# A depthwise convolution shared between the matrix engine and the vector engine

## The chip, the cores and the metric

The kernel runs on one core of a Trainium2 chip. A core has five engines with a queue of instructions each: TensorE (PE in the profile, its weight loads PEld), VectorE (DVE), ScalarE (ACT), GpSimd (POOL) and SyncE (SP), which here issues nearly all DMAs. Each queue runs in order, and engines wait for one another through semaphores. [...] The metric is the device time of one execution in microseconds; lower is better.

## The reference

A two-layer decoder trunk with width 2048, 256 positions, batch 1, all in float32:

```
layer 0: x <- LN(a*x + (1+gt)*S5(x*(1+sc)+sh));    x <- LN(a*x + (1+gt)*FFN(...))
layer 1: x <- LN(a*x + (1+gt)*Conv(x*(1+sc)+sh));  x <- LN(a*x + (1+gt)*FFN(...))

Conv(u):  ab = u @ w_pw1                      # 2048 -> 4096
          v  = ab[:, :D] * sigmoid(ab[:, D:])
          v[t, d] = sum_{k<31} v[t-30+k, d] * w_dw[k, d] + b_dw[d]   # causal, each channel alone
          v  = LayerNorm(v) ; return silu(v) @ w_pw2
FFN(u):   (silu(u @ w_g) * (u @ w_u)) @ w_down                      # 2048 -> 5632 -> 2048
```

The vectors sh, sc and gt, six per layer, come from a conditioning vector: `silu(c) @ ada_w[i] + ada_b[i]`, a matrix of 2048 x 12288 per layer. The change touches the 31-tap convolution in `Conv`, the LayerNorm behind it, and the time at which the products with `ada_w` are made.

## The kernel before

Activations lie with channels on the 128 partitions, in 16 chunks of 128 channels by 256 positions. A matmul in float32 precision is made of three faster ones: weights and activations are each split into a rounded part and the rest (`whi`, `wlo`; `hh`, `hl`), and hi x hi, hi x lo and lo x hi are summed. Weights arrive in units of four 128-row blocks by 512 columns (class `Unit`): SyncE loads `raw` (four buffers in all), ScalarE casts it to `whi` (L830), VectorE subtracts to make `wlo` (L831), PE multiplies (L886 with 512 output columns, L890 with 256). `gemm` runs one such unit after another; each is 24 or 48 matmuls.

**Modulation.** Most of `ada_w` goes through VectorE, not PE. A queue (`AdaQueue`) has one step per block: SyncE loads 1 MB into one of the same four buffers (`rawa`, L684), and VectorE adds it, times a column of `silu(c)`, to a running sum (`adaacc`, L699). Each unit of a gemm adds `ada.rate` to a credit; a whole credit starts a step, unless `ada.hold` is set. The credit starts at -3 behind a stage's first panel and never passes 1.5. `ada.finish` makes all steps that a vector still lacks. What remains of the last vector is made on PE (`ada_block`, L628).

**Convolution stage.** Eight gated gemms (i = 0 to 7) each yield two chunks, 2i and 2i+1. Gemms 0 to 6 come out with positions on partitions and are turned by PE (L902); the last one comes out with channels on partitions. `conv_in` copies both chunks with 30 zero columns ahead of them into `pad`, one of two tiles for pairs. PE has no operation per channel, so the convolution is put as matmuls over four shifted copies: SyncE writes `pad` to DRAM (`scr`, L1576) and reads it back four times (`conv_copies`, L1591) into `vs`, in which 32 channels stand four times, shifted by 0 to 3 positions. For the last gemm PE and two copying engines make `vs` without DRAM (`conv_spread`, L1598 to L1602). GpSimd makes the matching weights `lw` (L1581), 32 x 32 diagonals. `conv_out` then issues, for each chunk, 8 groups of 4 taps x 4 quarters of 32 channels (L1608: 32 matmuls in the program, 64 in the profile), and VectorE moves the result out of PSUM into `V`, with the bias added and the shift of the LayerNorm subtracted (L1617).

`Stats` collects the sums of `V` and of its squares: ScalarE squares (L764), VectorE adds both to running sums pair by pair (L773, L775); `finish` sums over partitions on PE (L790, L794), makes the inverse deviation on VectorE and spreads it on PE (L809). A stage opened with `apart` leaves the last pair out of the running sums and keeps it as `tail`.

**Swish.** `Feed` then drives the first gemm of `w_pw2`: for each pair, VectorE normalises (L818, L819), ScalarE makes the sigmoid (L1645) and the affine form (L947), GpSimd multiplies them (L1647), VectorE rounds the product to `hh` (L910, in `split3`), GpSimd makes the rest `hl` (L911). For the first pair VectorE does all but the rest (L1634 to L1638).

**Order of the work.** `later.put(n, f)` calls f when n further units have begun, so the program's text order interleaves convolution work with weight units. That order is not yet the queues' order: a planner with a cost model fills each engine's queue, taking what is ready in its model and, among that, what was written first. So work written later can be moved ahead. Only some PE stretches are set by hand, and `queue_behind` ties instructions behind a given one. `later.flush` behind gemm 7 calls all that is still due.

Of the kernel before, what the change touches and what calls it, by code (L numbers as in the profile page):

```python
# [11 lines left out]
F32 = mybir.dt.float32  # L12
# [14 lines left out]
CONV_G = 8  # L27
WIDTH = 31
# [477 lines left out]
def kernel(  # L506
# [231 lines left out]
    class Stats:  # L738
# [22 lines left out]
        def add(self, i, z):  # L761

            sq = self.sp.tile([P, 2, SEQ], F32, tag="lnsq", name="lnsq", bufs=2)
            act = nc.scalar.activation(out=sq, in_=z, func=AF.Square)  # L764
# [7 lines left out]
            a, b = self.first if i == 1 else (s[:, 0], s[:, 1])  # L772
            dve = nc.vector.tensor_tensor(out=s[:, 0], in0=a, in1=z, op=ADD)  # L773
            if i < 7:
                nc.vector.tensor_tensor(out=s[:, 1], in0=b, in1=sq, op=ADD)  # L775
            else:
                self.tail = sq
                self.marks = [dve, act]

        def finish(self, fill=None):  # L780
# [4 lines left out]
            sp, s, sq = self.sp, self.s, self.tail  # L785
# [5 lines left out]
            for k in range(2):  # L791
                for q in range(4):
                    t = slice(64 * q, 64 * q + 64)
                    mm = nc.tensor.matmul(b[32 * q:32 * q + 32, 64:P], ones[:, 0:32], sq[:, k, t], start=False, stop=k == 1)  # L794
# [113 lines left out]

    def split3(src, hi, lo):
        a = nc.vector.tensor_copy(out=hi, in_=src)  # L910
        nc.gpsimd.tensor_tensor(out=lo, in0=src, in1=hi.bitcast(F32), op=SUB)  # L911
        return [a]
# [596 lines left out]
    with mctx:  # L1509
# [39 lines left out]
        ada.rate, ada.behind = 0.71, True  # L1549
# [11 lines left out]
        for p in pad:  # L1561
            nc.vector.memset(p[:, :, :WIDTH - 1], 0.0)
            nc.vector.memset(p[:, :, LP - 1:], 0.0)
        dramp = cvctx.enter_context(tc.tile_pool(name="dram", bufs=1, space=bass.MemoryType.DRAM))
        scr = [dramp.tile([P, 2, LP], F32, name=f"scr{i}") for i in range(7)]
        cstats = Stats("cln", sp)
        ada.rate = 0.6

        def conv_in(i, t):
            p = pad[i % 2]  # L1570
            for k in range(2):
                nc.scalar.copy(out=p[:, k, WIDTH - 1:LP - 1].rearrange("p (c t) -> p t c", t=2), in_=t[:, k].rearrange("p (t c) -> p t c", t=2))
            vs = cp.tile([P, 2, 4, LS], F32, tag="vs", name="vs", bufs=2)
            wait = {0: 5, 7: 2}.get(i, 6)
            if i < 7:
                later.put(wait - 3, lambda: nc.sync.dma_start(scr[i], p))  # L1576
                later.put(wait - 2, lambda: conv_copies(scr[i], vs))
            for k in range(2):
                ch = 2 * i + k
# [3 lines left out]
                    in1=bc(wtap[:, :, 4 * ch:4 * ch + 4].rearrange("p g q -> p q g"), 3, 32), op=MUL)  # L1583
                if i == 7:
                    later.put(1 + k, lambda k=k: conv_spread(p[:, k], vs[:, k]))
                later.put(wait + k, lambda ch=ch, k=k, lw=lw: conv_out(ch, vs[:, k], lw))
# [125 lines left out]
```

## Time and profile before

| | us |
|---|---|
| median of three runs | 2320.72 |
| lowest and highest | 2317.39, 2323.02 |
| the profiled execution, its own time | 2323.75 |
| its span, first to last instruction | 2322.0 |

The stages that matter in its trace: feed-forward of layer 0 until about 1140 us from the start of the span, convolution from 1178 to 1438, its LayerNorm and swish until 1484, the rest of `w_pw2` until 1560, feed-forward of layer 1 behind that.

A row of groups reads: line, engine, operation, output <- inputs, shapes, count | busy us, mean ns of one | idle us just ahead of them, and what ended it. A row of the timeline reads: start us, duration us, engine, line, operation, count, and in brackets the idle time ahead and its releaser.

### The profile page before, as it was taken

The numbers are of one execution on the slowest core, as the hardware profiler recorded it, in microseconds if no ns is written. First come the engines' busy times: TensorE is split into PE (matmuls) and PEld (weight loads), VectorE is DVE, ScalarE is ACT, GpSimd is POOL, SyncE is SP. The second block draws the span as 40 slices with busy tenths as digits, with TensorE's granted clock in tenths as the row PEclk, the third lists the DMA queues.
The fourth block names the chain that finished last, engine by engine and source line by source line (L and its number), as shares of the span: only waits on it lengthen the run. The fifth ranks groups of instructions, "written<-read, shape, count | busy, mean of one in ns | idle before, by whom it ended". The sixth has DMA issues, their size and how long they took to land.

```text
span 2322.0 us, 33968 instructions
## 1 busy us (share of the span) xinstructions
PE 2249.4 (97%) x13905; PEld 1811.9 (78%) x13905; DVE 1633.0 (70%) x1778; ACT 1011.1 (44%) x1242; POOL 186.6 (8%) x283
## 2 busy tenths in 40 slices
PE   6888999999999999999999998999999999999998
PEld 4545778988888888888897676798888888888888
DVE  8899878887777777777885565788754544555564
ACT  4666335554333334344453322556434333334343
POOL 5662000000000000000011111400000000000000
PEclk9999999999999999999999999999999999999999
DMA  9889799589888898988757886766865556555542
GB/s 334 289 301 302 268 320 337 168 304 323 294 321 294 314 318 294 324 293 318 274 164 222 265 241 193 276 223 206 275 218 187 193 182 197 184 182 189 191 164 91
DMA packets 382307, 582.35 MB, mean 251 GB/s; under 512 B 13604, under 2 KB 279124, under 8 KB 367684
## 3 DMA queue, kind: packets, MB, share of 16 engines
q1 hardware_dynamic: 381718, 579.73, 73.8%
q8 instruction: 109, 1.79, 0.3%
q0 software_dynamic: 192, 0.37, 0.1%
q14 instruction: 48, 0.39, 0.0%
q10 hardware_dynamic: 240, 0.08, 0.0%
HBM read 575.97 MB, written 4.15 MB: 250 GB/s over the span
## 4 chain that ended last, share of the span: by engine, by line
PE 82%; DVE 8%; DMA 4%; ACT 3%; issue 1%; POOL 1%; SPq 0%; DVEq 0%; ACTq 0%; POOLq 0%
PE acc L886 67%; PE acc L890 5%; PE conv L1608 2%; DVE wlo L831 2%; PE acc L1007 2%; PE turned L902 2%; DMA raw<-in_cv_w_pw_dram 1%; DMA raw<-in_s_w_glu_dram 1%; ACT whi L830 1%; DVE pin L462 1%; PE y L499 1%; PE ada L628 1%; DMA raw<-in_ada_w_dram 1%; DVE adaacc L699 1%; DVE x L450 0%
## 5 line engine op out<-in xcount | busy, mean ns | idle before, releaser
L831 DVE TENSOR_TENSOR wlo<-raw,whi 128x2048 fp32r<-128x2048 f32 x344 | 795.6, 2313 | 491.0 <-ACT whi L830 490.6
L830 ACT CAST whi<-raw 128x2048 fp32r<-128x2048 f32 x344 | 655.0, 1904 | 805.0 <-PE acc L886 579.1
L886 PE MATMUL acc<-whi,h 128*128 128x512 f32 x3648 | 895.0, 395 | 10.8 <-ACT whi L830 10.5
L886 PEld LDWEIGHTS acc<-whi,h 128*128 128x128 f32 x3648 | 679.4, 188 | 169.7 <-ACT whi L830 16.4
L886 PE MATMUL acc<-wlo,h 128*128 128x512 f32 x1824 | 466.1, 392 | 2.8 <-DVE wlo L831 2.8
L886 PEld LDWEIGHTS acc<-wlo,h 128*128 128x128 f32 x1824 | 341.6, 188 | 81.3 <-DVE wlo L831 6.7
L886 PE MATMUL acc<-whi,f 128*128 128x512 f32 x1248 | 300.5, 391 | 0.0
L699 DVE SCALAR_TENSOR_TENSOR adaacc<-rawa,c_act,adaacc 128x2048 f32<-128x2048 f32 (+1 forms) x135 | 284.5, 2108 | 0.4
L886 PEld LDWEIGHTS acc<-whi,f 128*128 128x128 f32 x1248 | 233.0, 188 | 48.9 <-ACT whi L830 0.8
L886 PE MATMUL acc<-wlo,f 128*128 128x512 f32 x624 | 156.4, 389 | 0.0
L886 PEld LDWEIGHTS acc<-wlo,f 128*128 128x128 f32 x624 | 117.1, 188 | 24.3
L1581 POOL TENSOR_TENSOR lw<-fold,wtap 128x1024 f32<-128x1024 f32 x16 | 33.7, 2110 | 1146.4 <-PE acc L890 926.4
L628 PE MATMUL ada<-raw,c_rep 128*32 128x512 f32 (+1 forms) x576 | 72.5, 600 | 5.7 <-DMA raw<-in_ada_w_dram 3.2
L1240 ACT ACTIVATE fsg<-acc 128x256 f32<-128x256 f32 x84 | 31.7, 380 | 100.0 <-PE acc L886 100.0
L890 PEld LDWEIGHTS acc<-h,whi 128*128 128x128 f32 x512 | 62.1, 190 | 8.1 <-DVE h L1637 2.6
L890 PE MATMUL acc<-h,whi 128*128 128x256 f32 x512 | 65.7, 283 | 2.6 <-DVE h L1637 1.7
L1184 POOL CAST lnmh<-lno 128x2 fp32r<-128x2 f32 x1 | 0.2, 183 | 829.3 <-DVE lno L66 829.3
L1608 PE MATMUL conv<-vs,lw 128*32 128x256 f32 x1024 | 59.8, 380 | 0.0
L1608 PEld LDWEIGHTS conv<-vs,lw 128*32 128x32 f32 x1024 | 36.7, 110 | 20.9 <-issue 3.0
L1241 DVE TENSOR_TENSOR fsg<-acc,fsg 128x256 f32<-128x256 f32 x84 | 35.1, 420 | 19.9 <-ACT fsg L1240 19.8
L462 DVE TENSOR_TENSOR_SCAN pin<-rho,pin 128x256 f32<-128x256 f32 x64 | 44.3, 692 | 1.5
L1617 DVE SCALAR_TENSOR_TENSOR V<-conv,vec,shift 128x256 f32<-128x256 f32 x14 | 9.7, 693 | 48.8 <-PE conv L1608 48.8
(331 smaller groups left out, 1829.8 us busy)
## 6 DMA issues: line engine op xcount, KB each, us to landing
raw<-in_ffn_w_gu_dram SPq DMA_DIRECT2D x352, 512.0 KB, 4.5
rawa<-in_ada_w_dram SPq DMA_DIRECT2D x128, 1024.0 KB, 5.9
raw<-in_ffn_w_down_dram SPq DMA_DIRECT2D x88, 1024.0 KB, 5.1
raw<-in_ada_w_dram SPq DMA_DIRECT2D x64, 1024.0 KB, 7.8
raw<-in_s_w_glu_dram SPq DMA_DIRECT2D x64, 512.0 KB, 6.0
raw<-in_cv_w_pw_dram SPq DMA_DIRECT2D x64, 512.0 KB, 6.3
raw<-in_cv_w_pw_dram SPq DMA_DIRECT2D x16, 1024.0 KB, 5.6
vs<-scr SPq DMA_DIRECT2D x28, 284.0 KB, 7.4
```

The lines of the kernel that those rows point to most:

```text
L462: v.tensor_tensor_scan(out=z, data0=rh[:, a].rearrange("p r h c -> p (r h c)"), data1=z, initial=0.0, op0=MUL, op1=ADD)
L628: nc.tensor.matmul(acc[32 * (k % 4):32 * (k % 4) + 32, :], c_rep[:, kk, :], r[:, k, :], start=kk < 4, stop=kk >= NCH - 4)
L699: nc.vector.scalar_tensor_tensor(out=acc, in0=r[:, i], scalar=c_act[:, kk:kk + 1], in1=acc, op0=MUL, op1=ADD)
L830: m1 = nc.scalar.copy(out=self.hi[:, :kn], in_=r[:, :kn])
L831: m2 = nc.vector.tensor_tensor(out=self.lo[:, :kn], in0=r[:, :kn], in1=self.hi[:, :kn].bitcast(F32), op=SUB)
L886: nc.tensor.matmul(acc[bank].rearrange("p a b -> p (a b)"), x[:, bank * HALF:(bank + 1) * HALF], wt[:, k], start=first, stop=end)
L890: nc.tensor.matmul(acc[bank][:, i], wt[:, k, m * P:(m + 1) * P], x, start=first and i == 0, stop=end and i == 1)
L902: nc.tensor.transpose(b[:, o:o + HALF], u[t][:, c0 + k * P:c0 + (k + 1) * P], ident)
L1007: nc.tensor.matmul(acc[m][:, 0:EW], wt[:, k, m * P:(m + 1) * P], xx[:, 4 * u + k], start=u == 0 and n == 0, stop=u == 3 and n == len(order ...
L1241: nc.vector.tensor_tensor(out=t[:, i], in0=gv[:, 0], in1=t[:, i], op=MUL)
L1581: nc.gpsimd.tensor_tensor(out=lw, in0=fold32.unsqueeze(1).unsqueeze(1).broadcast_to([P, 4, CONV_G, 32]), in1=bc(wtap[:, :, 4 * ch:4 * ch + ...
L1608: nc.tensor.matmul(acc[32 * q:32 * q + 32, :], lw[:, q, g, :], vs[:, q, 4 * g:4 * g + SEQ], start=g == 0, stop=g == CONV_G - 1)
```

## The change

Chunks 3, 7, 11 and 13 are no longer convolved by PE; VectorE sums their 31 taps. Of chunk 15, PE keeps the first 2 of 8 groups (taps 0 to 7) and VectorE sums taps 8 to 30.

- `conv_taps` multiplies a shifted view of the padded chunk by a column of 31 tap weights and adds it to one of two alternating sums (`vacc` and the chunk's place in `V`), joins the two and subtracts the shift. The taps are handed out with `later`: 4 per unit for i = 1 and 3, 7 for i = 5, 9 for i = 6, all 23 at once for i = 7.
- For i = 1, 3 and 5 the tap chunk has a pad tile of its own (`vpad`, two of them), because its taps run on for eight units (five for i = 5). Only the other chunk of such a pair goes through DRAM. `vs` is now one tile per chunk, three buffers, where it was one per pair, two buffers; `conv_copies` issues four reads per chunk.
- The tap columns are loaded by GpSimd's queue at the stage's start (five pieces), turned by PE after five units, and lie in the stage's own pool, which closes with the stage.
- `cstats` is opened with `apart`; `there` adds a pair to the statistics when both its chunks are done, in whatever order. `finish` takes a tail of one or two tiles.
- In `swish`, GpSimd's product and rest move to VectorE; the rounding copy moves from VectorE to ScalarE for pairs 1 to 7 (`split` in place of `split3`).
- `ada.rate` goes from 0.71 to 0.77 in feed-forward 0 and from 0.6 to 0.25 in the convolution, where the queue is also held for gemms 6 and 7.

The core of the diff:

```diff
+V_CHUNKS = (3, 7, 11, 13, 15)
+V_FROM = 8
...
-        ada.rate, ada.behind = 0.71, True
+        ada.rate, ada.behind = 0.77, True
...
-        cstats = Stats("cln", sp)
-        ada.rate = 0.6
+        cstats = Stats("cln", sp, True)
+        ada.rate = 0.25
...
+        for n, cs in enumerate((V_CHUNKS[:4], V_CHUNKS[4:])):
+            r = rows_in("taps", [cv_w_dw[0][:, P * c:P * c + P] for c in cs], nc.gpsimd)
+            later.put(5, lambda n=n, cs=cs, r=r: tap_columns(n, cs, r))
...
-            vs = cp.tile([P, 2, 4, LS], F32, tag="vs", name="vs", bufs=2)
+            ch = 2 * i
+            mine = ch + 1 in V_CHUNKS
+            vs = [cp.tile([P, 4, LS], F32, tag="vs", name="vs", bufs=3) for _ in range(1 if mine and i < 7 else 2)]
             wait = {0: 5, 7: 2}.get(i, 6)
...
+            acc = cp.tile([P, SEQ], F32, tag="vacc", name="vacc", bufs=2)
+            todo = list(range(V_FROM if i == 7 else 0, WIDTH))
+            n = {5: 7, 6: 9, 7: 23}.get(i, 4)
+            for m in range(0, len(todo), n):
+                later.put(1 + m // n, lambda js=todo[m:m + n]: conv_taps(ch + 1, acc, z[1], js, todo[0], js[-1] == WIDTH - 1))
...
+        def conv_taps(ch, acc, z, js, begin, last):
+            w, sums = taps[ch], (acc, V[:, ch])
+            for j in js:
+                a = sums[j % 2]
+                if j == begin:
+                    nc.vector.tensor_scalar(out=a, in0=z[:, j:j + SEQ], scalar1=w[:, j:j + 1], scalar2=cb_col[:, ch:ch + 1], op0=MUL, op1=ADD)
+                elif j == begin + 1:
+                    nc.vector.tensor_scalar(out=a, in0=z[:, j:j + SEQ], scalar1=w[:, j:j + 1], scalar2=None, op0=MUL)
+                else:
+                    nc.vector.scalar_tensor_tensor(out=a, in0=z[:, j:j + SEQ], scalar=w[:, j:j + 1], in1=a, op0=MUL, op1=ADD)
+            if not last:
+                return
+            nc.vector.tensor_tensor(out=acc, in0=acc, in1=V[:, ch], op=ADD)
...
+        def conv_rest(vs, lw):
+            acc = aux("conv")[:, :SEQ]
+            conv_groups(acc, vs, lw, V_FROM // 4)
+            o, a, b = V[:, 15].rearrange("p (t c) -> p c t", t=2), *(x.rearrange("p (c t) -> p c t", t=2) for x in (acc, tail[0]))
+            nc.vector.tensor_tensor(out=o, in0=a, in1=b, op=ADD)
+            there(15)
+
+        def there(ch):
+            done.add(ch)
+            if ch ^ 1 in done:
+                cstats.add(ch // 2, V[:, ch & ~1:(ch | 1) + 1])
...
             for j in range(4):
-                nc.sync.dma_start(vs[32 * j:32 * j + 32], s[:, :, j:j + LS].rearrange("(q r) k t -> r k q t", q=4))
+                for k, v in enumerate(vs):
+                    nc.sync.dma_start(v[32 * j:32 * j + 32], s[:, k, j:j + LS].rearrange("(q r) t -> r q t", q=4))
...
         for i in range(8):
+            ada.hold = i > 5
...
-            nc.gpsimd.tensor_tensor(out=h, in0=h, in1=V[:, s2], op=MUL)
-            return [m1] + split3(h, hh[:, s2], hl[:, s2])
+            nc.vector.tensor_tensor(out=h, in0=h, in1=V[:, s2], op=MUL)
+            return split(h, hh[:, s2], hl[:, s2])
```

More of the change, by code (lines that the diff above doesn't have):

```diff
@@ L907, in split @@
         return a, nc.vector.tensor_tensor(out=lo, in0=src, in1=hi.bitcast(F32), op=SUB)
[L909 to L912, printed above, removed]
     class Feed:
@@ new lines, in conv_in @@
+                if k == 1 and mine:
+                    later.put(4, lambda v=v, lw=lw: conv_rest(v, lw))
+                else:
+                    later.put(wait + k, lambda k=k, v=v, lw=lw: conv_out(ch + k, v, lw))
+            if not mine:
+                return
[4 more added lines that the diff above has]
+                later.put(1 + m // n, lambda js=todo[m:m + n]: conv_taps(ch + 1, acc, z[1], js, todo[0], js[-1] == WIDTH - 1))
@@ L1661 @@
         feed = Feed(cstats, swish, fill())
+        ada.hold = False
         ada.finish(1, 2)
```

68 lines of the change are left out of this document (42 added, 26 removed).

## The prediction

> **What bounds the kernel now.** I read the page first, then the busy time by stage, then the groups and the chain of waits of the convolution and of the LayerNorm behind it.
>
> ```profile
> span 2322.0 us, 33968 instructions
> PE 2249.4 (97%) x13905; PEld 1811.9 (78%) x13905; DVE 1633.0 (70%) x1778; ACT 1011.1 (44%) x1242; POOL 186.6 (8%) x283
> ```
>
> TensorE is busy nearly everywhere, but not evenly. The windows view gives, for each stretch, its length, the busy time of PE, PEld, DVE, ACT and POOL, the granted TensorE clock, the DMA share and GB/s.
>
> ```profile
> 420.00:1140.00 720.00, 719.62 (x3360) 592.79 (x3359) 557.74 (x429) 303.40 (x268) 0.00 (x0) 1.00 0.85 298
> 1182.00:1382.00 200.00, 192.56 (x1376) 144.72 (x1375) 128.78 (x118) 82.11 (x103) 21.29 (x10) 1.00 0.76 228
> 1382.00:1438.00 56.00, 50.68 (x648) 41.60 (x646) 26.43 (x26) 13.39 (x18) 5.93 (x3) 1.00 0.72 216
> 1416.00:1438.40 22.40, 19.54 (x320) 14.47 (x320) 7.12 (x13) 3.89 (x9) 1.97 (x1) 1.00 0.55 111
> 1437.00:1440.00 3.00, 1.56 (x39) 1.01 (x42) 1.59 (x4) 0.79 (x2) 0.00 (x0) 0.85 0.03 5
> 1440.00:1444.00 4.00, 4.00 (x32) 1.22 (x24) 2.77 (x13) 0.00 (x0) 0.00 (x0) 0.68 0.42 115
> ...
> 1437.00:1484.00 47.00, 38.53 (x307) 28.52 (x308) 32.09 (x58) 25.09 (x39) 25.43 (x16) 0.93 0.71 249
> 1484.00:1560.00 76.00, 76.00 (x463) 66.78 (x461) 65.92 (x78) 37.52 (x43) 0.00 (x0) 1.00 0.72 251
> ```
>
> The first row is the feed-forward of layer 0: PE has no gap. The convolution (1182 to 1438) and the stage that feeds its result to the next matmul (1437 to 1484) have gaps: 7.4, 5.3 and 8.5 us. VectorE has room in the convolution: 26.4 of 56 us at its end, while the last row shows PE without a gap beside a VectorE that is 87% busy. So here PE's work is the bound, then the gaps.
>
> **Taps: what leaves PE.** The groups of the convolution (1178 to 1437) and single rows of the timeline:
>
> ```profile
> L831 DVE TENSOR_TENSOR wlo<-raw,whi 128x2048 fp32r<-128x2048 f32 x32 | 80.2, 2509 | 30.5 <-ACT whi L830 30.5
> ...
> L1608 PE MATMUL conv<-vs,lw 128*32 128x256 f32 x1024 | 59.8, 380 | 0.0
> L830 ACT CAST whi<-raw 128x2048 fp32r<-128x2048 f32 x31 | 58.9, 1901 | 58.5 <-DMA raw<-in_cv_w_pw_dram 36.1 <-PE acc L886 13.4 <-PE acc L1007 5.5
> L886 PE MATMUL acc<-wlo,h 128*128 128x512 f32 x192 | 49.7, 396 | 2.6 <-DVE wlo L831 2.6
> ...
> L1046 DVE SCALAR_TENSOR_TENSOR sg<-lnrep,ecol,sg 128x256 f32<-128x256 f32 x4 | 1.7, 477 | 0.0
> ```
> ```profile
> 1215.00 0.87 DVE L1046 SCALAR_TENSOR_TENSOR sg<-lnrep,ecol,sg 128x256 f32<-128x256 f32 x2
> ...
> 1301.26 2.13 PE L886 MATMUL acc<-wlo,h 128*128 128x512 f32 x8 [0.49 <-DVE wlo L831]
> ...
> 1310.52 2.12 PE L886 MATMUL acc<-whi,h 128*128 128x512 f32 x8 [1.64 <-ACT whi L830]
> ...
> 1318.50 3.95 PE L886 MATMUL acc<-whi,h 128*128 128x512 f32 x16 [1.59 <-ACT whi L830]
> ...
> 1356.89 7.11 PE L1608 MATMUL conv<-vs,lw 128*32 128x256 f32 x128
> ```
>
> Two chunks take 128 matmuls in 7.11 us, so one costs 3.55 us of PE. Chunks 3, 7, 11 and 13 leave whole, chunk 15 keeps 2 of its 8 groups: 4.75 chunks, 16.9 us. Chunks 3 and 7 lie wholly in the stretch up to 1382, where PE sets the pace: **7.1 us off**.
>
> The price is on VectorE: 4 x 31 + 23 = 147 taps, nearly all scalar_tensor_tensor of 128x256. The L1046 row is the same form (SBUF in, scalar column, summed in place): 0.48 us each, but two in 0.87, so a new one starts each 0.40 us. 147 x 0.40 = 59 us; if each waited for the one before it, 147 x 0.48 = 71 us. The two alternating sums leave no tap waiting for its neighbour, so I take 0.40.
>
> **Room for them.** The modulation sums (adaacc) leave the stage. Their queue's credit rule, walked through the loops, gives 79 steps in feed-forward 0 and 13 in the convolution, as the trace has them:
>
> ```profile
> L684 SPq DMA_DIRECT2D rawa<-in_ada_w_dram x79: 340/341/341, 451.7 to 1120.9; - x79
> L699 DVE SCALAR_TENSOR_TENSOR adaacc<-rawa,c_act,adaacc x74: 2341/2345/2349, 481.6 to 1135.2; 128x2048 f32<-128x2048 f32 x74
> ...
> L684 SPq DMA_DIRECT2D rawa<-in_ada_w_dram x13: 340/546/2676, 1209.8 to 1381.0; - x13
> ```
>
> With the new rates the same walk gives 89 and 2; about as many as before follow later (13 against 12). The convolution loses 11 x 2.34 = 26 us of VectorE and 11 loads of 1 MB from SyncE's queue. Those loads share four buffers with the weights. Both 1.6 us gaps above are PE waiting for a cast that waited for a late weight load; with the buffers freer I take **2 us** of these 3.2. Against it, taps queue ahead of wlo: PE already waits 0.49 us for wlo at 1301, so a batch of four (1.6 us) can cost that where it meets a busy VectorE. Bounds +4 to -4 us of gain. On SyncE's queue 40 column copies of one chunk replace 28 of two, 12 issues more beside 11 loads less: nothing. GpSimd, idle for most of the stage, makes 12 of the 16 weight tiles lw and issues five small loads ahead of them, and VectorE clears two more pads: nothing that PE waits for.
>
> In feed-forward 0 the ten extra sums are 23 us in 720 on an engine 77% busy: 81%, below the 87% at which PE ran without a gap. Ten loads of 1 MB raise 298 GB/s by some 15. That cover is what hides them: **0**, and 23 us if it were gone.
>
> **The last matmul and what follows (1382 to 1438).**
>
> ```profile
> 1416.86 0.43 DVE L1093 TENSOR_TENSOR sg<-acc,sg 128x256 f32<-128x256 f32 x1 [0.76 <-ACT sg L1092]
> ...
> 1417.84 0.45 DVE L1602 COPY vs<-spread 128x284 f32<-128x284 f32 x1 [0.56 <-PE spread L1598]
> ...
> 1436.24 0.66 DVE L1617 SCALAR_TENSOR_TENSOR V<-conv,vec,shift 128x256 f32<-128x256 f32 x1 [2.76 <-PE conv L1608]
> 1436.94 0.63 ACT L764 ACTIVATE lnsq<-V 128x512 f32<-128x512 f32 x1 [6.25 <-DVE V L1617]
> ...
> 1437.60 0.69 DVE L775 TENSOR_TENSOR cln_s<-cln_s,lnsq 128x512 f32<-128x512 f32 x1
> 1438.44 0.65 PE L790 MATMUL lnsum<-cln_s,ones 128*32 128x128 f32 x16 [2.23 <-DVE cln_s L775]
> ```
>
> Today PE works through the last chunks after the gate's last product (ends 1417.3); the sums begin at 1438.4. PE loses 2.75 chunks here, 9.8 us, but VectorE becomes the limit. Behind 1417.3 it owes 23 taps (9.2), their closing sum and shift (0.34 + 0.69), the join of chunk 15 (0.69), four copies (4 x 0.45), two results (2 x 0.69) and two sums (2 x 0.69): 15.5 us, so 1432.8 instead of 1438.3, 5.5 us earlier. If the last 13 taps of chunk 13 (5.2 us) are still owed, nothing is left. I take 1.5 here, and 2.5 of chunk 11's 3.55 us, since its and chunk 13's taps fill VectorE in the last matmul: **4 us**, with PE's 9.8 as the upper bound. The lower one: 35 taps come due in the four units of the last matmul and 36 behind it, 71 x 0.40 = 28.4 us, plus 1.9 of closings; VectorE is idle 29.6 us in this stretch. Where no gap takes them, they lie on the path: see the first rival.
>
> The last pair's statistics no longer pass VectorE (0.69 x 2 give way to a square of 0.63 and eight matmuls like the 0.65 us row's), and the columns cost PE two transposes, which I put at the size of that row as well: **-0.5** together.
>
> **The swish stage (1437 to 1484).** GpSimd's product and residue go to VectorE, the rounding copy to ScalarE.
>
> ```profile
> L911 POOL TENSOR_TENSOR h<-hf,h 128x512 fp32r<-128x512 f32 x7 | 13.1, 1870 | 3.8 <-DVE h L910 3.8
> L1647 POOL TENSOR_TENSOR hf<-hf,V 128x512 f32<-128x512 f32 x7 | 11.1, 1580 | 1.2 <-ACT V L947 1.2
> ...
> L1645 ACT ACTIVATE hf<-V,vec 128x256 f32<-128x256 f32 x14 | 7.7, 594 | 7.3 <-POOL h L911 5.2 <-DVE V L819 2.1
> L947 ACT ACTIVATE V<-V,vec 128x256 f32<-128x256 f32 x14 | 7.7, 589 | 0.0
> ...
> L819 DVE TENSOR_TENSOR V<-V,lnrep 128x512 f32<-128x512 f32 x7 | 4.8, 685 | 0.1
> L818 DVE TENSOR_TENSOR V<-V,lnrep 128x512 f32<-128x512 f32 x7 | 4.8, 680 | 0.0
> L910 DVE CAST h<-hf 128x512 fp32r<-128x512 f32 x7 | 3.0, 427 | 10.5 <-POOL hf L1647 10.5
> ```
> ```profile
> 1452.19 1.27 POOL L1647 TENSOR_TENSOR hf<-hf,V 128x512 f32<-128x512 f32 x1 [1.17 <-ACT V L947]
> ...
> 1476.60 3.28 POOL L911 TENSOR_TENSOR h<-hf,h 128x512 fp32r<-128x512 f32 x1 [0.54 <-DVE h L910]
> ...
> 1478.77 1.19 PE L890 MATMUL acc<-h,wlo 128*128 128x256 f32 x8 [1.46 <-DVE wlo L831]
> ```
>
> GpSimd is the slowest link: seven pairs from 1452.2 to 1479.9, 24.2 us of it busy. Afterwards a pair costs ScalarE 0.59 x 4 + 0.63 (the square of this size) = 3.0 us by durations (2.6 with the overlap of neighbours, as in the 0.87 row) and VectorE four operations of 0.68 (2.4 to 2.7). Seven pairs and three weight casts of 1.9: 24 us from 1450, so the last residue stands at about 1475 instead of 1479.9. PE has work beside it, so I take **3 us**; bounds 6 and, as VectorE gains 7.5 us of work in front of the wlo that PE waits 1.46 us for, -2.
>
> **The sum** against the execution's own 2323.75 us: 7.1 + 2 + 4 - 0.5 + 3 = 15.6, so 2308.1. That execution lies 3.0 above the median of the runs, so against 2320.72 it is **2305 us**.
>
> **The rivals.** *The taps land on the path of the last matmul.* VectorE's queue runs in order. In gemm 7 each wlo that PE waits for stands behind up to 12 taps, and behind it chunk 15's result stands behind what is left of chunk 13's. At worst 14.0 us (35 taps) delay wlo; behind the product come 36 taps and closings (16.3) on top of today's chain, less two results and their waits (2 x 0.69 + 2 x 2.76 = 6.9): 9.4. Together 23.4, against gains of 7.1 + 3.55 + 2 + 3 = 15.6: 7.8 slower, **2328 us**. It decides from the point where more than 39 of those 71 taps stand before something that PE waits for. For it: waits on conv like the 2.76 us one already hold VectorE there. Against it: 29.6 us idle, 4.7 more without two modulation sums, and a planner that moves ready work forward.
>
> *The gaps take all of it:* PE's 16.9 us, 4 of waits, 5 in the swish stage: 26, **2295 us**. For it stands VectorE's room, against it the tail's 15.5 us.
>
> *The weights set the pace:* the cast waits 36.1 us for loads. If matmuls come to wait where PE did convolution, the 7.1 and the 4 go, swish alone remains, less its half: **2319 us**. Against it: 11 MB of loads less.
>
> *A cold array.* PE idles 1.4 us of the three in 1437 to 1440 and is then granted 0.68.
>
> ```profile
> 1439.10 5.34 PE L628 MATMUL ada<-raw,c_rep 128*32 128x512 f32 x32
> ```
>
> If VectorE's tail leaves PE idle for longer, these 32 matmuls run at half clock: 5.34 x 0.68 / 0.5 = 7.3, 2 us more, and lnrep behind them 1 more: **2308 us**. [...]
>
> **How the numbers follow.** Chances: forecast 0.55, taps on the path 0.15, gaps take all 0.11, weights 0.11, cold array 0.08. Faster by over 0.2% (4.6 us, about what a measurement of this kernel tells from no change): forecast, full gain and cold array, plus a little of the weights' case, 0.76; within, 0.10; slower, 0.14. The range reaches from the full gain, 2295, to just short of the weights' case, 2317.
>
> **What would show it.** The conv group falls from 1024 matmuls to 720 and from 59.8 us to about 43. The tap line shows 147 operations of 0.48 us or less. adaacc counts 2 in the convolution and 89 before it. PE's gaps in the stretch that was 1182 to 1382 stay at or below 7.4 us, and the stretch is some 9 us shorter. From gemm 7's first unit to lnsum it takes about 52 us; 60 or more and the first rival holds. In the swish stage POOL is idle and the last residue comes some 3 to 5 us earlier. The forecast is wrong if PE's waits for wlo in the convolution exceed the 2.6 us of today's group by more than 5, or if feed-forward 0 shows PE gaps.

## The result, and the profile after

The changed kernel takes **2300.04 us** (median of four runs, 2298.67 to 2303.70) against 2320.21 (2317.39 to 2323.02) for the kernel before: a ratio of 0.9916, with a 95% interval from 0.9898 to 0.9933. The forecast was 2305 with a range from 2295 to 2317. The total was near; the table shows that its parts were not, so that the total came so near is in part luck.

The page of the kernel after begins so:

```profile
span 2299.0 us, 33563 instructions
PE 2230.6 (97%) x13619; PEld 1798.1 (78%) x13619; DVE 1691.5 (74%) x1945; ACT 1015.0 (44%) x1249; POOL 156.6 (7%) x268
```

I cut both traces at the same landmarks: the first matmul of feed-forward 0's and of the convolution's entry panel, the first unit of gemm 7 (the first weight matmul with 256 columns), `lnsum`, and the first `shift` matmul behind the swish stage. The windows view has the columns of the prediction; first before, then after:

```profile
419.50:1171.10 751.60, 751.22 (x3619) 624.12 (x3618) 578.03 (x453) 318.35 (x283) 0.00 (x0) 1.00 0.84 295
1171.10:1382.58 211.48, 203.53 (x1486) 155.12 (x1485) 140.26 (x129) 86.64 (x109) 27.77 (x13) 1.00 0.73 218
1382.58:1438.40 55.82, 50.10 (x645) 41.14 (x643) 26.15 (x26) 13.39 (x18) 5.93 (x3) 1.00 0.70 213
```
```profile
416.10:1176.70 760.60, 756.44 (x3631) 623.13 (x3630) 597.94 (x464) 318.44 (x284) 0.00 (x0) 1.00 0.88 306
1176.70:1369.36 192.66, 191.16 (x1348) 151.03 (x1346) 157.88 (x221) 88.28 (x109) 21.52 (x10) 1.00 0.69 201
1369.36:1416.90 47.54, 41.60 (x472) 31.60 (x469) 40.78 (x80) 11.84 (x17) 5.39 (x2) 0.96 0.33 105
```

| stage, us | before | after | change | forecast |
|---|---|---|---|---|
| S5 layer and what lies ahead (code not changed) | 419.5 | 416.1 | -3.4 | 0 |
| feed-forward 0 | 751.6 | 760.6 | **+9.0** | 0 |
| convolution up to gemm 7 | 211.5 | 192.7 | **-18.8** | -9.1 |
| gemm 7 to `lnsum` | 55.8 | 47.5 | **-8.3** | -3.5 |
| LayerNorm and swish | 45.0 | 44.3 | -0.7 | -3 |
| rest of `w_pw2`, feed-forward 1 | 838.6 | 837.8 | -0.8 | 0 |

The first row moves with every execution: over the profiles of this study, whose code there is the same, it lies between 411.4 and 419.5. The changes in the table add up to -23.0 us, by the medians it is -20.2. So a stage difference of a few us in one execution says little by itself; the medians decide.

Two errors of opposite sign nearly cancel: feed-forward 0 pays 9 us that I had put at nothing, and the convolution gains 27.1 us where the forecast had 12.6. The waits of ScalarE's weight casts in feed-forward 0 (us in total, times, longest), before and after, show a change of kind:

```profile
ACT whi L830 <- DMA raw<-in_ffn_w_down_dram: 13.5, 4, 4.7
...
ACT whi L830 <- DMA raw<-in_ffn_w_gu_dram: 6.0, 2, 4.3
```
```profile
ACT whi L833 <- DMA raw<-in_ffn_w_gu_dram: 158.4, 55, 6.2
...
ACT whi L833 <- DMA raw<-in_ffn_w_down_dram: 66.0, 21, 5.9
```

Before, a cast waited for a load in 6 cases; after, it does in 76. Yet PE is marked busy for 756.4 of 760.6 us. Matmul ends are modelled in these profiles, so I take it that a slightly late start need not show as idle: of the 9.0 us only 3.8 appear as more idle time, and PE's busy time grows by 5.2. Of these, 1.6 are 12 more matmuls, which sum up the extra modulation steps (`adar` 5.3 us against 4.3, `adat` 3.0 against 2.4); the other 3.6 come with the same work. Here **the stage's length and the casts' waits** tell what the busy share hides.

The convolution's groups after the change:

```profile
L834 DVE TENSOR_TENSOR wlo<-raw,whi 128x2048 fp32r<-128x2048 f32 x32 | 74.6, 2333 | 21.4 <-ACT whi L833 21.3
...
L833 ACT CAST whi<-raw 128x2048 fp32r<-128x2048 f32 x32 | 60.9, 1904 | 63.0 <-PE acc L889 34.9 <-issue 12.1 <-PE acc L1005 5.6
L889 PE MATMUL acc<-wlo,h 128*128 128x512 f32 x192 | 48.8, 391 | 0.0
L1667 PE MATMUL conv<-vs,lw 128*32 128x256 f32 x720 | 43.4, 390 | 2.5 <-DVE V L1680 2.0 <-DVE vs L1662 0.4
...
L701 DVE SCALAR_TENSOR_TENSOR adaacc<-rawa,c_act,adaacc 128x2048 f32<-128x2048 f32 x2 | 4.7, 2346 | 0.0
```

The row of L833 shows where a part of the gain comes from: the cast, which waited 36.1 us for weight loads, now waits mainly for PE to free its buffer. PE waits nowhere for wlo in the wide gemms (0.0 in the row of L889).

### The profile page after: what moved, and what is told of

Same layout as the page of the kernel before. It is cut to its first block, busy times and chain, and to the rows that moved or that the text cites. A ratio compares the mean times of both kernels' runs of the same rounds, so it can differ in the third digit from the quotient of the medians.

```text
span 2299.0 us, 33563 instructions
## 1 busy us (share of the span) xinstructions
PE 2230.6 (97%) x13619; PEld 1798.1 (78%) x13619; DVE 1691.5 (74%) x1945; ACT 1015.0 (44%) x1249; POOL 156.6 (7%) x268
## 4 chain that ended last, share of the span: by engine, by line
PE 71%; DVE 14%; DMA 8%; ACT 5%; issue 2%; SPq 0%; DVEq 0%; ACTq 0%
PE acc L889 57%; PE acc L893 5%; DMA raw<-in_ffn_w_gu_dram 4%; DVE wlo L834 4%; ACT whi L833 3%; DMA raw<-in_ffn_w_down_dram 2%; PE acc L1005 2%; DVE adaacc L701 2%; PE conv L1667 1%; PE turned L905 1%; DVE pin L464 1%; PE y L501 1%; DMA raw<-in_s_w_glu_dram 1%; PE ada L630 0%; DVE x L452 0%
## 5 line engine op out<-in xcount | busy, mean ns | idle before, releaser
L834 DVE TENSOR_TENSOR wlo<-raw,whi 128x2048 fp32r<-128x2048 f32 x344 | 789.1, 2295 | 465.1 <-ACT whi L833 462.2
L833 ACT CAST whi<-raw 128x2048 fp32r<-128x2048 f32 x344 | 655.2, 1905 | 821.4 <-PE acc L889 447.1
L889 PE MATMUL acc<-whi,h 128*128 128x512 f32 x3648 | 895.5, 394 | 5.4 <-ACT whi L833 5.1
L889 PEld LDWEIGHTS acc<-whi,h 128*128 128x128 f32 x3648 | 677.8, 188 | 164.6 <-ACT whi L833 12.7
L889 PE MATMUL acc<-wlo,h 128*128 128x512 f32 x1824 | 465.5, 392 | 0.8 <-DVE wlo L834 0.6
L889 PEld LDWEIGHTS acc<-wlo,h 128*128 128x128 f32 x1824 | 341.9, 188 | 78.1 <-DVE wlo L834 3.4
L889 PE MATMUL acc<-whi,f 128*128 128x512 f32 x1248 | 301.1, 391 | 0.1
L889 PEld LDWEIGHTS acc<-whi,f 128*128 128x128 f32 x1248 | 232.7, 188 | 50.1 <-ACT whi L833 2.2
L889 PE MATMUL acc<-wlo,f 128*128 128x512 f32 x624 | 156.6, 389 | 0.2 <-DVE wlo L834 0.2
L889 PEld LDWEIGHTS acc<-wlo,f 128*128 128x128 f32 x624 | 117.0, 188 | 24.9 <-DVE wlo L834 0.6
L1594 POOL TENSOR_TENSOR lw<-fold,wtap 128x1024 f32<-128x1024 f32 x12 | 26.9, 2249 | 1060.5 <-PE acc L893 870.9
L1667 PE MATMUL conv<-vs,lw 128*32 128x256 f32 x720 | 43.4, 390 | 2.5 <-DVE V L1680 2.0
L464 DVE TENSOR_TENSOR_SCAN pin<-rho,pin 128x256 f32<-128x256 f32 x64 | 44.3, 692 | 1.5
L893 PE MATMUL acc<-f,whi 128*128 128x256 f32 x320 | 40.7, 284 | 0.0
L1667 PEld LDWEIGHTS conv<-vs,lw 128*32 128x32 f32 x720 | 22.9, 112 | 21.8 <-issue 5.0
```

Of the source, the lines that this page charges most:

```text
L464: v.tensor_tensor_scan(out=z, data0=rh[:, a].rearrange("p r h c -> p (r h c)"), data1=z, initial=0.0, op0=MUL, op1=ADD)
L833: m1 = nc.scalar.copy(out=self.hi[:, :kn], in_=r[:, :kn])
L834: m2 = nc.vector.tensor_tensor(out=self.lo[:, :kn], in0=r[:, :kn], in1=self.hi[:, :kn].bitcast(F32), op=SUB)
L889: nc.tensor.matmul(acc[bank].rearrange("p a b -> p (a b)"), x[:, bank * HALF:(bank + 1) * HALF], wt[:, k], start=first, stop=end)
L893: nc.tensor.matmul(acc[bank][:, i], wt[:, k, m * P:(m + 1) * P], x, start=first and i == 0, stop=end and i == 1)
L1594: nc.gpsimd.tensor_tensor(out=lw, in0=fold32.unsqueeze(1).unsqueeze(1).broadcast_to([P, 4, CONV_G, 32]), in1=bc(wtap[:, :, 4 * (ch + k):4 ...
```

## The experiments

Times are medians; the kernel before, run beside these, stood at 2318.9 to 2320.8. Stage times are of the one profiled execution, which lies 7 us above the median of its kernel for taps_back, 6 above for ffn0_half_sums, 10 above for conv_small_loads and 10 below for spread, and within 5 us of it for the others.

### Which part of the change earns the time

Four kernels: the rates alone on the kernel before (rates_only); the whole change with the old rates (rates_old); the whole change with the swish stage's product and rest back on GpSimd and the rounding back on VectorE (swish_old); the whole change with all chunks back on PE (taps_back).

The diff shows them in this order; rates_old reverses the rates' lines on the kernel after, and taps_back also gives `vs` a fourth buffer in the place of the second pads.

```diff
-        ada.rate, ada.behind = 0.71, True
+        ada.rate, ada.behind = 0.77, True
-        ada.rate = 0.6
+        ada.rate = 0.25
+            ada.hold = i > 5
...
-            nc.vector.tensor_tensor(out=h, in0=h, in1=V[:, s2], op=MUL)
-            return split(h, hh[:, s2], hl[:, s2])
+            nc.gpsimd.tensor_tensor(out=h, in0=h, in1=V[:, s2], op=MUL)
+            return [m1] + split3(h, hh[:, s2], hl[:, s2])
...
-V_CHUNKS = (3, 7, 11, 13, 15)
+V_CHUNKS = ()
```

> The kernel before with the three rate edits alone (0.77 in feed-forward 0, 0.25 and the hold in the convolution). Theory A (the convolution's surplus over the prediction came from the taps themselves: PE's matmuls and the gaps round them): feed-forward 0 takes about 9 us more, the convolution only about 4 less, so some 5 us slower than before, 2325. Theory B (the surplus came from moving the modulation sums out of the convolution): feed-forward 0 also 9 more, the convolution 12 or more less, so about 3 faster, 2317. The prediction on record had feed-forward 0 at 0 and the convolution at 2 less: 2318.

> The changed kernel with the old rates (0.71, 0.6, no hold): taps and swish alone. Theory A: feed-forward 0 returns to about 753 us, 9 less, the convolution takes 4 to 5 more, so about 2296, faster than the change. Theory B: the convolution takes 12 or more longer, so 2303 or above.

> The changed kernel with GpSimd's product and residue back in the swish stage. Both theories: from the first sums to the next gemm the changed kernel took 45.3 us against 46.0, so no more than 1 us slower, about 2301. By the prediction's step it would be 3 slower, 2303.

> The changed kernel with no chunk on VectorE: PE convolves all sixteen; new rates, new swish and the statistics with the last pair apart stay (column copies one chunk each, four buffers, no extra pads). Theory A: about 23 us slower than the change, 2323. Theory B: the taps are worth what PE loses less some stalls, about 13, so 2313.

| | whole | ratio to before (95%) | feed-forward 0 | convolution |
|---|---|---|---|---|
| before (profiled first) | | | 751.6 | 267.3 |
| rates_only | 2319.81 | 1.0000 [0.9988, 1.0011] | 762.6 | 256.6 |
| rates_old | 2323.64 | 1.0018 [1.0007, 1.0028] | 751.5 | 276.3 |
| taps_back | 2316.51 | 0.9989 [0.9974, 1.0003] | 762.6 | 256.6 |
| swish_old | 2299.71 | 0.9919 [0.9901, 0.9938] | 756.7 | 241.0 |
| after | 2300.04 | 0.9916 [0.9898, 0.9933] | 760.6 | 240.2 |

Both theories fall as they were put, since neither part earns anything alone; B, which gave the larger share to moving the sums, was nearer in the three runs that part them. The new rates by themselves take 11 us from the convolution and add 11 to feed-forward 0, with no net effect. The taps (with the swish edit, but without the rates) make the convolution 9 us longer, though 16.9 us of work leave PE. Only together do they pay: under the new rates the taps take 256.6 to 240.2 us, 16.4 us, which is nearly all of PE's 16.9; the medians of taps_back and of the kernel after differ by 16.5. The convolution of rates_only, to be held against the two rows of the kernel after:

```profile
1177.00:1433.60 256.60, 251.65 (x2118) 192.23 (x2116) 141.88 (x142) 99.79 (x126) 33.64 (x16) 1.00 0.64 182
```

The swish edit is worth nothing that these runs can tell (2299.71 against 2300.04).

What the rates do in the convolution stands in one row of waits each; the first is of rates_only, the second of the kernel before:

```profile
ACT whi L830 <- DMA raw<-in_cv_w_pw_dram: 4.9, 1, 4.9
```
```profile
ACT whi L830 <- DMA raw<-in_cv_w_pw_dram: 36.1, 10, 8.4
```

### Why feed-forward 0 pays

How much it pays differs from one execution to the next: at the old rates the six profiled executions of this study show 751.5 or 751.6 us for the stage, at the new pace six others, whose code there is that of the kernel after or of low_spread below, show 756.7 to 762.6. So the price lies between 5 and 11 us, and 9.0 is one draw.

Two kernels on the one after: the modulation steps of feed-forward 0 load half the bytes while VectorE's sum keeps its 2048 columns (it reads the loaded half twice), or load everything while VectorE sums half (`('sum', 1024)` in the first line).

```diff
-        ada.rate, ada.behind = 0.77, True
+        ada.rate, ada.behind = 0.77, True; ada.cut = ('load', 1024)
...
+            m = c if what == "load" else n
             nc.sync.dma_start(
-                r, ada_w[layer, k * rows * P:(k + 1) * rows * P, j * D + 512 * b0:(j + 1) * D].rearrange("(k p) n -> p k n", p=P))
+                r[:, :, :m], ada_w[layer, k * rows * P:(k + 1) * rows * P, j * D + 512 * b0:j * D + 512 * b0 + m].rearrange("(k p) n -> p k n", p=P))
...
+                o, x = acc, r[:, i]
+                if what == "load":
+                    o, x = acc.rearrange("p (a c) -> p a c", c=c), r[:, i, :c].unsqueeze(1).broadcast_to([P, n // c, c])
+                elif what == "sum" and kk:
+                    o, x = acc[:, :c], r[:, i, :c]
```

> The kernel after, but in feed-forward 0 each modulation step loads only half of its block (1024 of 2048 columns, 0.5 MB instead of 1 MB) and VectorE's sum reads that half twice, so that it stays 2048 wide; the modulation vectors made there are therefore not the reference's. Theory D, the loads are what feed-forward 0 lost 9 us to (the DMA share rose from 0.84 to 0.87, and ScalarE's casts waited 158 us for weight loads instead of 6): the stage falls from 760.6 to 752 us or less, and the whole to about 2291. Theory V, it is VectorE's time (583 to 603 us busy): the stage stays at 760 us and the whole at about 2300.

> The kernel after, but in feed-forward 0 each modulation step loads its whole 1 MB and VectorE sums only 1024 of the 2048 columns; the vectors are again not the reference's. Some 89 x 1.17 = 104 us of VectorE's time leave the stage. Theory D (loads): the stage stays near 760 us, the whole near 2300, less what an earlier freed buffer gives. Theory V (VectorE's time): the stage falls to 752 us or less and the whole to about 2291.

Half the bytes: 2294.79 us (0.9879 [0.9863, 0.9896]), stage 755.4. Half the sums: **2308.53** us (0.9943 [0.9920, 0.9965]), stage **771.7**, longer than with whole sums; single runs of it reach from 2301.58 to 2314.06, and the profiled one is the slowest. The loads of the stage, KB each and median us from issue to landing, in the kernel before, in the kernel after, with half the loads and with half the sums:

```profile
raw<-in_ffn_w_gu_dram SPq DMA_DIRECT2D x166, 512.0 KB, 4.6
rawa<-in_ada_w_dram SPq DMA_DIRECT2D x79, 1024.0 KB, 5.5
```
```profile
rawa<-in_ada_w_dram SPq DMA_DIRECT2D x89, 1024.0 KB, 5.5
raw<-in_ffn_w_gu_dram SPq DMA_DIRECT2D x166, 512.0 KB, 5.1
```
```profile
raw<-in_ffn_w_gu_dram SPq DMA_DIRECT2D x166, 512.0 KB, 4.7
rawa<-in_ada_w_dram SPq DMA_DIRECT2D x89, 512.0 KB, 4.1
```
```profile
rawa<-in_ada_w_dram SPq DMA_DIRECT2D x89, 1024.0 KB, 6.9
raw<-in_ffn_w_gu_dram SPq DMA_DIRECT2D x166, 512.0 KB, 6.0
```

Theory V falls: 86 us less of VectorE's work do not shorten the stage; in the profiled executions it is 11 us longer, by the medians the kernel is 8.5 us slower. Theory D holds in its direction: fewer bytes bring back 5.2 us, by the stage and by the medians alike, and a weight load lands in 4.7 us, nearly as before the change (4.6). The stage alone would not show this, since 755.4 is only 1.3 us below the lowest of the six above. What the stage's length goes with is the time for which the casts wait for loads: 20 us in the kernel before, 40 in rates_old (751.5), 150 with half the bytes, 198 to 232 in the six, 274 with half the sums.

Why less work on VectorE makes the weights land later (6.0 us) no run isolates. My reading is that a buffer that is freed earlier lets the next 1 MB start earlier, and that the slower sums had spaced the loads out; the mean DMA share is no higher for it (0.87 against 0.88). Why half the bytes do not bring back the rest stays open too. The steps hold buffers that the weights also need, whatever their size, and no run gave them buffers of their own; and the planner orders the queues anew for each of these kernels.

It is the pace that counts, not the number. The kernel low_spread below ran feed-forward 0 at the new rate and stopped at 79 steps, the number of the kernel before:

```profile
414.10:1173.90 759.80, 754.27 (x3619) 623.53 (x3618) 576.62 (x453) 318.05 (x283) 0.00 (x0) 1.00 0.84 292
```

The stage still took 759.8 us, with the mean DMA share of before (0.84) and no more VectorE time than before (576.6 us against 578.0). While the steps ran, the share stood higher; the same hundred us in low_spread and in the kernel before:

```profile
540.00:640.00 100.00, 98.30 (x442) 79.24 (x441) 77.17 (x52) 40.49 (x34) 0.00 (x0) 1.00 0.93 326
```
```profile
540.00:640.00 100.00, 100.00 (x454) 81.22 (x453) 75.09 (x54) 39.69 (x34) 0.00 (x0) 1.00 0.88 309
```

### Why the old rates spoil the taps

In rates_old the convolution has 147 taps and 13 sums. PE's longest wait there (9.19 us) and what VectorE did ahead of it, from the timeline:

```profile
1352.47 1.91 ACT L833 CAST whi<-raw 128x2048 fp32r<-128x2048 f32 x1 [1.20 <-DVE vacc L1625]
1352.69 0.48 DVE L1625 SCALAR_TENSOR_TENSOR vacc<-vpad,taps,vacc 128x256 f32<-128x256 f32 x1
...
1366.41 0.47 DVE L1625 SCALAR_TENSOR_TENSOR vacc<-vpad,taps,vacc 128x256 f32<-128x256 f32 x1
...
1368.32 2.27 DVE L834 TENSOR_TENSOR wlo<-raw,whi 128x2048 fp32r<-128x2048 f32 x1
...
1370.64 3.49 PE L889 MATMUL acc<-wlo,h 128*128 128x512 f32 x8 [9.19 <-DVE wlo L834]
```

The cast is done at 1354.4, but the wlo that needs only it starts at 1368.3: between this wlo and the one before it stand 31 taps in VectorE's in-order queue. Two more such piles hold 24 and 23. In the kernel after no pile ahead of the last gemm's end is over 18, and PE's longest wait for wlo is 0.6. Three single remedies and one pair, all on rates_old. conv_small_loads has the first edit (256 of 2048 columns are loaded, the sums stay whole), conv_small_sums the same with `('sum', 256)`, rates_old_spread the second (each batch of taps up to chunk 13 is tied behind the newest unit's wlo), and small_loads_spread both:

```diff
-        ada.rate = 0.6
+        ada.rate = 0.6; ada.cut = ('load', 256)
...
-            for j in js:
-                a = sums[j % 2]
+            with queue_behind(newest.marks[1:] if behind else []):
+                for j in js:
+                    a = sums[j % 2]
```

> The taps, the swish edit and the old rates (0.71; 0.6, no hold), with the convolution stage's modulation steps loading 256 of 2048 columns (an eighth of the bytes) while VectorE's sum stays 2048 wide; those vectors are not the reference's. With whole loads this kernel needs 276.3 us for the convolution and 2323.6 in all. Theory Q, taps and sums in VectorE's one queue make the weights late: the convolution stays at 270 us or more and the whole at about 2320. Theory L, the loads of 1 MB crowd the weights' loads: the convolution falls to about 245 us and the whole to about 2295.

> As the run with small loads, but with the convolution stage's modulation steps loading all of their bytes while VectorE sums only 256 of 2048 columns; those vectors are not the reference's. Theory Q (VectorE's queue): the convolution falls from 276.3 to about 245 us and the whole from 2323.6 to about 2293. Theory L (loads): the convolution stays at 270 us or more and the whole at about 2320.

> The taps, the swish edit and the old rates, as the run that needs 276.3 us for the convolution and 2323.6 in all, with one thing else: each batch of taps of chunks 3, 7, 11 and 13 is tied behind the wlo of the newest weight unit, so that at most 12 taps stand ahead of any wlo, where 31, 24 and 23 did. Same work, same bytes, same rates. Theory O, the pile of taps in VectorE's in-order queue is what made the weights late: PE's waits for wlo in the convolution fall from 15.7 us to under 4, the stage to about 250 us and the whole to about 2300. Theory F, VectorE and the loads are simply too full with 13 sums and 147 taps in the stage, in whatever order: the stage stays at 270 us or more, the whole at 2318 or more.

> Both remedies at once on the kernel with taps and old rates (276.3 us for the convolution, 2323.6 in all): the taps tied behind the newest wlo (alone 265.3 us, 11.0 less) and the stage's modulation steps loading an eighth of their bytes (alone 259.7, 16.6 less; VectorE's sums stay whole, and those vectors are not the reference's). Theory A, the pile of taps and the loads are two causes that add: 276.3 - 11.0 - 16.6 = about 249 us for the stage, 2296 in all. Theory V, VectorE's own work is the floor under both: it is busy 223 us in each of these kernels, 86% of the 259.7, which is as full as it gets anywhere in this kernel (87% in the rest of w_pw2): the stage stays at 256 us or more and the whole at about 2304.

| on rates_old | whole | ratio to before (95%) | convolution | DVE busy |
|---|---|---|---|---|
| nothing | 2323.64 | 1.0018 [1.0007, 1.0028] | 276.3 | 223.4 |
| small loads | 2306.03 | 0.9937 [0.9912, 0.9962] | 259.7 | 223.5 |
| small sums | 2317.68 | 0.9983 [0.9971, 0.9996] | 266.7 | 201.3 |
| taps tied | 2315.99 | 0.9976 [0.9964, 0.9989] | 265.3 | 220.9 |
| small loads and taps tied | 2308.46 | 0.9943 [0.9924, 0.9962] | 257.9 | 223.2 |

Each remedy brings back a part of the 36.1 us that lie between 276.3 and the 240.2 of the kernel after, and none comes near all. Theories Q, L, O and F all named one cause, and none fits. Tying the taps is the cleanest of the runs, since it changes neither work nor bytes nor rates: PE's waits for wlo in the wide gemms fall from 15.7 us to 3.3, as theory O had it (6.9 are left in the last gemm, where 3.6 stood), but the stage only by 11.0, where O wanted 26. A part of the 36.1 us is not idle time: in rates_old PE is busy 242.7 us against 232.8 in the kernel after, with 16 matmuls more and at a granted clock of 0.95 against 0.99. Cutting the sums left the piles where they were (31, 24 and 21 taps), and PE's wait with them: 15.7 us for wlo in three times, as in rates_old.

```profile
PE acc L889 <- DVE wlo L834: 15.7, 3, 9.2
```

Small loads had shrunk the piles as well (23 and 10 at most in the wide gemms), presumably because the planner's cost model then expects the weights earlier. So the two together do not add: 257.9 us and 2308.46, where theory A wanted 249 and 2296. (The profiled execution with small loads alone lies 10 us above its median, so its 259.7 may be some us long; by the medians tying adds nothing to small loads.)

```profile
1166.40:1424.30 257.90, 242.25 (x1832) 186.62 (x1831) 223.17 (x312) 100.43 (x127) 30.63 (x12) 0.97 0.57 168
```

What theory V of that run forecast came: with piles and bytes gone the stage stays at 257.9 us, VectorE 87% busy, while the DMA share is only 0.57. Of PE's 15.6 us of waits there, 13.6 end with an instruction of VectorE. With two sums VectorE owes 199 us instead of 223, and then PE's 233 are the longer bill (240.2 in all). That VectorE's work is the floor is the best reading rather than a proof: a run with short sums and tied taps together would show it, and was not made, and the lower clock (0.97 against 0.99) is in the 257.9 as well, by an estimate from these two shares with some 5 us.

### Towards a better version

If pace spoils feed-forward 0 and order spoils the convolution, tied taps might allow ten sums to return. spread ties the taps of the kernel after and changes nothing else; low_spread also gives the convolution 12 sums.

```diff
-            while self.credit >= 1.0 and not self.hold:
+            while self.credit >= 1.0 and not self.hold and len(self.todo) > self.floor:
-        ada.rate, ada.behind = 0.77, True
+        ada.rate, ada.behind, ada.floor = 0.77, True, 25
-        ada.rate = 0.25
+        ada.rate, ada.floor = 0.75, 0
```

> The kernel after, with the batches of taps of chunks 3, 7, 11 and 13 tied behind the wlo of the newest weight unit; the longest piles ahead of a wlo before gemm 7 fall from 16 and 14 taps to 8 and 14 (two sums are all that is left in the stage). Theory O: PE idles 5.9 of 224 us in this stage up to the last gemm, so at most that is to be had: 240.2 becomes 236 to 240 us, and 2300 becomes 2296 to 2300. Theory F: no change, 2300.

> The kernel after with the tied taps, and with ten of the modulation steps back in the convolution: 79 steps in feed-forward 0 (a floor under the queue stops them there), 12 in the convolution at a rate of 0.75, none in gemms 6 and 7. Theory O: feed-forward 0 returns to 751.5 us (9 less than the kernel after), the convolution needs 245 to 250 us, the whole about 2296. Theory F: the convolution needs 260 us or more, the whole 2308 or more.

spread: 2301.61 us (0.9914 [0.9882, 0.9946]), convolution 239.3: no different from the kernel after. low_spread: 2320.47 us (1.0002 [0.9988, 1.0015]), with 759.8 us in feed-forward 0 (the pace, above) and 264.6 in the convolution. Theory F holds there: twelve sums are too many beside the taps even without piles (at most 12 taps stand ahead of any wlo of the stage). No version that computes the reference is clearly faster than the changed kernel; what the change chose, nearly all sums out of the stage, is what makes its taps pay.

## Why the prediction came out right, and where it was wrong

**Feed-forward 0, "0, and 23 us if it were gone": wrong, 9 us.** I bounded it by VectorE's load (81%, under the 87% that PE survives elsewhere), and VectorE is not what ends last there; the run with half the sums shows that, since the stage does not shorten with 86 us less of VectorE. The row that mattered stood in my own fence: a DMA share of 0.85 and 298 GB/s. I raised it by "some 15" GB/s and asked nothing further of it. The price was between my 0 and my 23, and the convolution's larger gain covered it: that is the luck in the total.

**Late weight loads, "2 us of these 3.2": mis-sized, 10.7 us.** I counted the two gaps that PE shows. The casts' 36.1 us of waits were the better measure; rates_only removes 31.2 of them, and the stage is 10.7 us shorter with no tap moved. Not all of it need be the loads: PE's waits there fall from 11.4 us to 2.6, of them 3.9 for casts, 3.6 for wlo and 2.5 for `pad` that are gone, and rates_only takes 24.5 us off VectorE as well as the loads. No run parts the two.

**Taps up to gemm 7, "7.1 us off", and the last matmul, "4 us", with "-0.5" for columns and statistics: mis-sized, together 16.4.** Behind 1382 I credited only 4 of the 9.8 us that PE loses. Under the new rates nearly all 16.9 us came, 10.6 being what the forecast counted: against rates_only, whose gemm 7 begins at 1379.34, it is 9.7 us up to gemm 7 (7.1 forecast) and 6.7 behind (3.5). From gemm 7's first unit to `lnsum` it takes 47.5 us, where I said about 52. The tail in the timeline after:

```profile
1369.36 2.89 PE L893 MATMUL acc<-h,whi 128*128 128x256 f32 x23
...
1398.29 0.42 DVE L1091 TENSOR_TENSOR sg<-acc,sg 128x256 f32<-128x256 f32 x1
...
1399.20 0.41 DVE L1621 TENSOR_SCALAR vacc<-pad,taps,vec 128x256 f32<-128x256 f32 x1
...
1401.34 0.48 DVE L1625 SCALAR_TENSOR_TENSOR V<-pad,taps,V 128x256 f32<-128x256 f32 x1
1401.74 0.48 DVE L1625 SCALAR_TENSOR_TENSOR vacc<-pad,taps,vacc 128x256 f32<-128x256 f32 x1
...
1409.18 5.93 PE L1667 MATMUL conv<-vs,lw 128*32 128x256 f32 x80 [2.00 <-DVE V L1680]
...
1414.32 0.69 DVE L1680 SCALAR_TENSOR_TENSOR V<-conv,vec,shift 128x256 f32<-128x256 f32 x1 [3.89 <-PE conv L1667]
...
1416.92 0.65 PE L792 MATMUL lnsum<-cln_s,ones 128*32 128x128 f32 x16 [1.81 <-DVE cln_s L778]
```

All of chunk 13's taps are done before the gate's last product (1398.3 to 1398.7), so no older debt stood in the way, and the 15.5 us of VectorE's bill were near: it is busy for 14.0 us there. But the bill left out that VectorE in turn waits for PE's last convolution (3.89 us at 1414.32), so the stretch behind the product takes 18.2 us instead of 21.1, 2.9 less and not 5.5; the other 5.4 of the 8.3 us lie ahead of the product. A tap starts each 0.40 us, as I took it.

**The swish stage, "3 us": wrong, nothing.** The last residue came 41.4 us behind `lnsum` in both kernels (1479.9 - 1438.4 before). After:

```profile
1453.50 1.90 ACT L833 CAST whi<-raw 128x2048 fp32r<-128x2048 f32 x1
...
1455.31 0.61 ACT L909 CAST h<-hf 128x512 fp32r<-128x512 f32 x1
1455.44 2.29 DVE L834 TENSOR_TENSOR wlo<-raw,whi 128x2048 fp32r<-128x2048 f32 x1 [1.24 <-ACT whi L833]
...
1457.65 0.68 DVE L910 TENSOR_TENSOR h<-hf,h 128x512 fp32r<-128x512 f32 x1
```

The last pair's rounding stands behind a 1.90 us weight cast on ScalarE, and its rest behind a 2.29 us wlo on VectorE: the work left GpSimd for two engines on which the weights go first. My sum had the casts in it, but not in the chain of the last pair. This is a reading of these rows; swish_old shows only that the edit is worth nothing.

**What was to show it.** As said: 720 matmuls and 43.4 us in the conv group, 2 sums in the stage and 89 ahead of it, GpSimd idle in the swish stage, PE's gaps up to gemm 7 at 1.5 us. Otherwise than said: feed-forward 0 shows PE gaps (4.2 us, 3.8 more than before), which I had named as a sign against the forecast, and which it was; and the taps' groups average 0.48 to 0.54 us, which four taps of 1.35 to 2.20 us raise (see the last section).

**The rivals.** *Taps on the path* was the right mechanism at the wrong place and under another condition: not gemm 7, but a pile of 31 in a wide gemm, and only where the sums stay. The forecast had set both edits' prices apart and added them; the runs show that the taps' price hangs on the rates, -16.4 or +9.0. *The gaps take all* came nearest in the convolution (16.4 of its 16.9 us, and 10.7 with the rates where it had 4), and failed in the swish stage (0.7 of its 5). *The weights set the pace* struck feed-forward 0 instead: there the casts wait for loads. *The cold array* did not strike the modulation matmuls: they ran in 3.64 us instead of 5.34. No run shows the rival's own term, half clock for all 32 (7.3 us) once PE idles for longer. In the kernel before the clock stood at 0.50 from 1439.1 to 1442.5, 3.4 of those 5.34 us, behind a gap of 2.23 us. In rates_only a gap of 2.29 us stands ahead of the same matmuls, and they take 3.64 us:

```profile
1433.63 0.64 PE L790 MATMUL lnsum<-cln_s,ones 128*32 128x128 f32 x16 [2.29 <-DVE cln_s L775]
...
1434.29 3.64 PE L628 MATMUL ada<-raw,c_rep 128*32 128x512 f32 x32
```

But in the kernel after the 80 matmuls of the last two chunks did run at 0.76, from 1409.2 on:

```profile
1398.70:1409.18 10.48, 7.50 (x105) 3.27 (x97) 10.34 (x28) 1.51 (x4) 0.00 (x0) 0.98 0.01 2
1409.18:1415.20 6.02, 5.93 (x80) 2.82 (x80) 2.10 (x6) 0.15 (x1) 0.00 (x0) 0.76 0.01 4
...
1417.80:1421.44 3.64, 3.64 (x47) 1.10 (x35) 2.71 (x13) 0.22 (x1) 0.00 (x0) 1.00 0.35 86
```

At 3.55 us for 64 they would take 4.4 us, so by this estimate it cost 1.5. PE's longest gap ahead of the slow stretch is 2.00 us, in a stretch where it is 72% busy. Finer windows show where the clock fell:

```profile
1405.25:1408.67 3.42, 1.41 (x17) 0.32 (x16) 3.42 (x10) 0.40 (x1) 0.00 (x0) 1.00 0.00 0
1408.67:1412.08 3.41, 2.90 (x28) 1.38 (x32) 1.76 (x5) 0.00 (x0) 0.00 (x0) 0.50 0.02 7
```

The granted clock was 0.50 for 3.4 us, behind 3.4 us in which PE was busy for 1.41. What sets it no run isolates.

## What to carry to other kernels

Price two edits together when they load the same in-order queue: each was worth nothing or less alone, and 20 us together. Look for the engine or path that the cover would run out on, not for the one that gets the work: VectorE had room for ten more sums in feed-forward 0 (it is 79% busy there with them), and the loads had not (the casts waited for one 76 times instead of 6). A busy share near 100% with modelled ends can hide time (here some 3.6 us of 760); compare stage lengths and the waits one step upstream.

## What the hardware showed that I had not expected

Less work on an engine made a stage slower: with half the sums, feed-forward 0 went from 760.6 to 771.7 us in the profiled executions, as the loads went from 5.1 and 5.5 us to 6.0 and 6.9. By the medians the kernel lost 8.5 us, though the fastest of its six runs (2301.58) lies among those of the kernel after.

Four taps beside a GpSimd operation lasted until 0.3 us behind its end. VectorE, then GpSimd, in the kernel after:

```profile
1304.43 1.84 DVE L1625 SCALAR_TENSOR_TENSOR V<-vpad,taps,V 128x256 f32<-128x256 f32 x1
1306.19 0.47 DVE L1625 SCALAR_TENSOR_TENSOR vacc<-vpad,taps,vacc 128x256 f32<-128x256 f32 x1
...
1312.07 2.28 DVE L834 TENSOR_TENSOR wlo<-raw,whi 128x2048 fp32r<-128x2048 f32 x1
```
```profile
1304.01 1.98 POOL L1594 TENSOR_TENSOR lw<-fold,wtap 128x1024 f32<-128x1024 f32 x1 [24.26 <-PE conv L1667]
1313.32 2.87 POOL L1594 TENSOR_TENSOR lw<-fold,wtap 128x1024 f32<-128x1024 f32 x1 [7.33 <-PE conv L1667]
```

The tap of 1304.43 ends at 1306.27, 0.3 us behind the end of the weights' making at 1305.99, and lasts 1.84 us instead of 0.47. The other way round, the making of 1313.32 meets the wlo that runs from 1312.07 to 1314.35 and takes 2.87 us instead of 1.98. The four, of 147 taps, lost some 5 us in all in the profiled execution of the kernel after. That the GpSimd operation is the cause is my reading of such rows; no run isolates it.
